# A hybrid encoder step: input in two pieces with weights between, the pool mixer's products one group later, parameters turned inside a chunk

## The chip, the cores and the metric

The kernel runs on one core of one Trainium2 chip, as one launch. The metric is the device time of an execution in microseconds (us), the median of several runs. Beside it stands one profiled execution, whose trace is read here: its span runs from the first to the last instruction.

## The reference

One layer of a streaming encoder trunk, for 256 prompt frames of a new stream and 32 frames of a running one (288 positions in all), model width 2048, in float32:

```python
def run_layer(x, pos, hist_pool, hist_sconv, h0, hist_fconv, p):
    xn = rmsnorm(x, p['norm_mix_pre'])
    proj = xn @ p['w_in']
    u, z, xbc, dt_raw = proj[..., :o1], proj[..., o1:o2], proj[..., o2:o3], proj[..., o3:]
    y_pool, new_pool = pool_mixer(u, ...)    # 4 groups of 256 channels, trailing means over 2/4/8/16
    y_ssd, new_sconv, new_h = ssd_mixer(z, xbc, dt_raw, ...)   # conv, chunked scan, gate, grouped norm
    mix = jnp.concatenate([y_pool, y_ssd], axis=-1) @ p['w_out']
    x = x + rmsnorm(mix, p['norm_mix_post'])
    up, new_fconv = causal_dwconv(rmsnorm(x, p['norm_ffn_pre']) @ p['w_up'], ...)
    gate, val = up[..., :D_FF], up[..., D_FF:]
    f = (jax.nn.silu(gate) * val) @ p['w_down']
    return x + rmsnorm(f, p['norm_ffn_post']), new_pool, new_sconv, new_h, new_fconv
```

In the pool mixer each group takes its trailing mean less `u` and multiplies it by a 256 x 256 matrix, `y = einsum('bsgc,gcd->bsgd', d, w_pool)`. The outputs are the new frames and the states.

## The kernel before

Activations lie transposed, channels on the 128 partitions and the 288 positions along the row. A K tile is 128 input channels; there are 16 of them at the input. Each weight and each activation is split into a high and a low part, and one product of the mathematics is three on TensorE (PE): high x high, high x low, low x high (`mm3`, L162 to L164). ScalarE (ACT) makes the high part of a weight (`whi`, L156), VectorE (DVE) the low part (`wlo`, L157), four buffers each.

The instructions of each engine run in order. A planner that models the engines sets that order, except for the instructions marked `pin` or `keep_in_program_order`, which hold the order of the program; `high_priority` moves an instruction ahead in the plan.

**The head.** The 800 columns of `w_in` that are needed first (some `u`, B, C and dt) are computed chunk by chunk over K: `CHUNKS` has ten chunks, c0 to c3 of one K tile each and c4 to c9 of two. The first four K tiles come in by rows and are turned on PE (`turn_first`). The other twelve come in three pieces of four K tiles (`input_load(1)` to `(3)`, L238, four loads each, one for each 32 partitions), with rows of 128 words, and the sample rows in four loads (L262). Channels are dealt to K tiles with a step of four (`j=4`), so that DVE can turn a tile from these pieces (L386). All these loads and the weights of a chunk (`first_load`, two loads, L244 and L245) are issued by one engine, SP, in the order of the program: c0, c1, c2, c3, input piece 1, sample rows, c4, c5, input pieces 2 and 3, c6 to c9.

`prepare(i)` makes chunk i ready: on ACT the high part of the weights (L382, L383), the high part of `xn` (L391), and for some chunks squares of the input (L417); on DVE the turned input (L386), the low part of the weights (L396) and of `xn` (L398). It is called one chunk ahead. Then come the chunk's products (L483): 20 for a chunk of one tile, 40 for one of two.

In front of the products of c5, c6 and c7 a block of parameters is turned on PE (`columns`, L328) and copied by ACT (L434, L437, L440); the FFN's parameters are turned before products 0 and 24 of c8 (L475). All these use one buffer in turn, since the other two of its pool hold sums: a turn waits for the copy of the one before.

**The pool mixer.** Projections of 256 columns follow one another (`project`, 96 products). At the end of the mixer stage:

```python
for n, i in enumerate((2, 1, 0)):
    ps = ups.pop() if n == 0 else project(win, [(256 * i, 256)], xn, K16)
    for j in range(2):
        pool_in(2 * i + j, ps[j])
    pool_tile(2 * i + 2)
    pool_tile(2 * i + 3)
    pool_group(i + 1)
    for t in range(8 + 3 * n, min(11 + 3 * n, NX)):
        tc.keep_in_program_order(dve.tensor_tensor(xs[t], xs[t], rg[1], op=ALU.mult))
```

`pool_in` takes a projection's result out of PE's memory, `pool_tile` makes the window sums and the split `du` on DVE and ACT (L884 to L891, L120, L121), and `pool_group` multiplies two `du` tiles by the group's matrix (12 products) and splits the result for the output projection (L124, L125). Beside this runs the norm factor `rg[1]` of the second SSD group (a square root, L768, and a reciprocal, L769). The output projection starts with the SSD's tiles (`mixs`) and ends with the pool's (`mixp`).

Of the kernel before, what the change touches and what calls it, by code (L numbers as in the profile page):

```python
# [8 lines left out]
F32 = mybir.dt.float32  # L9
# [7 lines left out]
P = 128  # L17
# [3 lines left out]
NS = 32  # L21
# [28 lines left out]
def body(  # L50
# [57 lines left out]
    def aux(shape, name):  # L108
        return aux_ps.tile(shape, F32, tag="aux", name=name)
# [115 lines left out]
    xsv = x_sample.rearrange("o t (c i w) -> i (o t) c w", i=4, w=P)  # L225
# [9 lines left out]

    def input_load(c):
        for i in range(4):
            pin(sp.dma_start(out=xt[NS * i : NS * (i + 1), 0:8, c - 1, :], in_=xpv[i][:, :, c, :]))  # L238

    def first_load(kb, n):  # L240

        raw = wpool.tile([P, n, NW], F32, tag="raw", name="raw")
        src = win0[:, kb : kb + n] if kb < 4 else win[:, kb // 4, kb % 4 : kb % 4 + n]
        pin(sp.dma_start(out=raw[:, :, 2 * P :], in_=src[:, :, O_B : O_B + NW - 2 * P]))  # L244
        pin(sp.dma_start(out=raw[:, :, : 2 * P], in_=src[:, :, D_POOL - 2 * P : D_POOL]))  # L245
        raws.append(raw)
# [41 lines left out]
    for i in range(NE):  # L288
# [2 lines left out]
        ebuf.append(e)  # L291

    pool.dma_start(
        out=g_mix_pre[:, 4:].rearrange("p (c j) -> p c j", j=4),
        in_=norm_mix_pre[0, 4 * P :].rearrange("(c p j) -> p c j", p=P, j=4),
    )
    ubuf = []
    for i in range(4):
# [36 lines left out]

    xn = []
    xT = []
    xT_d = dram.tile([4, P, 4, NT], F32, name="xT_d")
# [15 lines left out]
    spots = xin.tile([P, 9, NS], F32, name="spots")  # L354
    pf = const.tile([P, 6, NF * 2], F32, name="pf")
    copies = []
    last_split = []

    def turn_first(t):
# [7 lines left out]
    def prepare(i, p_=None):  # L367

        kb, n = CHUNKS[i]
        raw = raws.pop(0)  # L370

        w = xin.tile([P, n, 2 * NW + HEADS], F32R, tag="w", bufs=3, name="w")
        hi, lo = w[:, :, :NW], w[:, :, NW : 2 * NW]
        tiles = range(kb, kb + n)
        pieces = (slice(2 * P, 4 * P), slice(4 * P, NW), slice(0, 2 * P)) if i == 0 else (slice(0, NW),)
        for t in tiles:
            xT.append(btile("xT"))
            xn.append(atile("xn"))
        if i == 0:
            pin(act.activation(xn[0][:, 0, :], p_, AF.Copy, scale=g_mix_pre[:, 0:1]))  # L380
        for c in pieces:
            pin(act.activation(hi[:, :, c], raw[:, :, c], AF.Copy))  # L382
        pin(act.activation(w[:, :, 2 * NW :], raw[:, :, NB:], AF.Copy))  # L383
        for t in tiles:
            if p_ is None:
                pin(dve.transpose(  # L386
                    xT[t].rearrange("p (b t) -> p b t", t=NS),
                    xt[:, :, t // 4 - 1, :].rearrange("p b (f j) -> p b f j", j=4)[:, :, :, t % 4],
                ))
            if i:  # L390
                pin(act.activation(  # L391
                    xn[t][:, 0, :], xT[t] if p_ is None else p_, AF.Copy, scale=g_mix_pre[:, t : t + 1]
                ))
        if i:
            for c in pieces:
                pin(dve.tensor_tensor(lo[:, :, c], raw[:, :, c], hi[:, :, c].bitcast(F32), op=ALU.subtract))  # L396
        for t in tiles:
            pin(dve.scalar_tensor_tensor(  # L398
                xn[t][:, 1, :], xT[t] if p_ is None else p_, g_mix_pre[:, t : t + 1], xn[t][:, 0, :].bitcast(F32),
                op0=ALU.mult, op1=ALU.subtract,  # L400
            ))
        if p_ is not None:
            for c in pieces if i == 0 else ():
                pin(dve.tensor_tensor(lo[:, :, c], raw[:, :, c], hi[:, :, c].bitcast(F32), op=ALU.subtract))
            pin(dve.tensor_copy(xT[kb], p_))
        if i + 4 < len(CHUNKS):
            first_load(*CHUNKS[i + 4])
        if i == 1:
            input_load(2)
            input_load(3)  # L410
        if 1 <= i <= 3:
            b = i - 1
            src = x0[:, b] if b < 2 else x0s
            n_ = src.shape[0]
            pin(act.activation(junk[:n_], src, AF.Square, accum_out=ssum[:n_, 9 + b : 10 + b]))
        for b in SQUARES.get(i, ()):
            pin(act.activation(  # L417
                junk[:, : 3 * P].rearrange("p (c w) -> p c w", w=P), xt[:, b], AF.Square, accum_out=ssum[:, b : b + 1]
            ))
        return w  # L420

# [6 lines left out]
    for i, (kb, n) in enumerate(CHUNKS):  # L428
        if 4 <= i + 1 < len(CHUNKS):
            ahead_w.append(prepare(i + 1))  # L430

        if i == 5:
            pb = columns(pb_in, 108, "pb", copies)
            pin(act.activation(*copies.pop(), AF.Copy))  # L434
        if i == 6:
            pa = columns(pa_in, 124, "pa", copies)
            pin(act.activation(*copies.pop(), AF.Copy))  # L437
        if i == 7:
            pc = columns(pc_in, 120, "pc", copies)
            pin(act.activation(*copies.pop(), AF.Copy))  # L440
        if i == len(CHUNKS) - 1:

            pool.tensor_tensor(
# [25 lines left out]
        for q, (r, m, k, x) in enumerate(products):  # L469
            if i < 3 and q == (6 if i else 12):  # L470
                ahead_w.append(prepare(i + 1, turn_first(i + 1)))
            if i == 8 and q in (0, 24):
                p_ = aux([P, 3, NF * 2], "ptf")
                for j in range(3):
                    pin(pe.transpose(p_[:, j, :], pf_in[:, q // 8 + j, :], ident[: NF * 2, : NF * 2]))  # L475
                pin(act.activation(pf[:, q // 8 : q // 8 + 3, :], p_, AF.Copy))
# [6 lines left out]
            pin(pe.matmul(out, c, xn[kb + k][:, x, :], start=kb + k + r + x == 0, stop=kb + k == KD - 1 and stop))  # L483
    early.close()
    ahead[0] = 200
    g_mix_post = pb[:, 60:76]
    g_ffn_pre = pb[:, 76:92]
    g_ffn_post = pb[:, 92:108]
# [66 lines left out]
        pool_in(NU - 2 + i, first[i])  # L555

    xs_ps = [project(win, [(O_X, 256)], xn, K16, wait=last_split)]
    xT_f = xT_d.rearrange("c p j n -> (c p j) n")
    for t in range(KD):
        pin(sp.dma_start(out=xT_d[t // 4, :, t % 4, :] if t > 3 else xT_f[t * P : (t + 1) * P, :], in_=xT[t]))  # L560
    xs_in = {}


# [446 lines left out]
    for grp in ((0, 1), (2,), (3,), (4,), (5,), (6,), (7,)):  # L1010
# [7 lines left out]
        elif grp[0] == 6:  # L1018
            late_in[:] = [state_in(t, t >= LATE + 4) for t in range(LATE, NX - 2)]
        if grp[0] == 0:  # L1020
            sp.dma_start(out=xT, in_=xT_d.rearrange("c p j n -> (c p j) n").rearrange("(k q) n -> q k n", q=P))
# [334 lines left out]
```

## Time and profile before

| what | value |
|---|---|
| median of 3 runs | 1366.51 us (1365.96 to 1369.6) |
| profiled execution, its own time | 1366.29 us |
| its span | 1364.6 us |
| mean granted TensorE clock | 0.994 |
| PE / DVE / ACT / POOL busy | 98% / 65% / 49% / 17% |
| bytes moved by DMA, mean rate | 252.15 MB, 185 GB/s |

A row of the timeline is: start and length in us, engine, line, operation, output and inputs, count, and in brackets the idle time before it and what ended it. The granted clock is the share of full speed at which TensorE ran. A line number is that of the kernel before; a helper's line stands for all its callers, so the names of tiles tell them apart.

### The profile page before, as it was taken

What the parts mean: (1) busy time and instruction counts of PE and PEld (TensorE: products, weight loads), DVE (VectorE), ACT (ScalarE), POOL (GpSimd) and SP (SyncE); (2) the same over time, 40 slices, a digit from 0 to 9 for tenths busy, and PEclk for the clock granted to TensorE, in tenths of its full rate; (3) what the DMA queues carried; (4) which work ended last, traced back from release to release, by engine and by line L of the source; (5) the groups of instructions that cost most, each with busy time, mean ns of one, the idle gap of its engine ahead of it and who ended that gap; (6) DMA issues with size and microseconds to landing.
All of it is one profiled execution on the core that took longest, in us unless ns stands there. A gap on an engine that the chain in (4) does not pass through costs nothing.

```text
span 1364.6 us, 25783 instructions
## 1 busy us (share of the span) xinstructions
PE 1340.9 (98%) x10183; PEld 1329.1 (97%) x10183; DVE 892.5 (65%) x1510; ACT 671.7 (49%) x1029; POOL 231.9 (17%) x395
## 2 busy tenths in 40 slices
PE   8999999989999999999999999999999999999997
PEld 7999999979999999999999999999999999999996
DVE  6799979768634469977766643335666666664444
ACT  5656957535444356644444443334444444454442
POOL 4121112211232330211211100000211111101110
PEclk9999999999999999999999999999999999999999
DMA  9879887555755654877555455555455554576763
GB/s 260 253 199 256 242 247 205 149 163 180 228 174 183 184 153 139 251 198 198 168 160 181 147 170 170 160 168 175 156 173 167 161 176 158 166 233 179 199 172 91
DMA packets 302945, 252.15 MB, mean 185 GB/s; under 512 B 74708, under 2 KB 295410, under 8 KB 302822
## 3 DMA queue, kind: packets, MB, share of 16 engines
q1 hardware_dynamic: 300414, 245.76, 59.8%
q0 software_dynamic: 2352, 4.66, 1.2%
q8 instruction: 80, 1.31, 0.4%
q14 instruction: 43, 0.35, 0.1%
q10 hardware_dynamic: 56, 0.07, 0.0%
HBM read 236.13 MB, written 14.31 MB: 184 GB/s over the span
## 4 chain that ended last, share of the span: by engine, by line
PE 90%; DMA 5%; DVE 2%; SPq 1%; issue 1%; ACT 1%; DVEq 0%; ACTq 0%
PE acc L162 28%; PE acc L164 28%; PE acc L163 28%; DMA xs_d<-blocks 2%; PE acc L483 1%; DMA xk<-xs_d 1%; PE pst L986 1%; DMA raw<-in_w_in 1%; DMA xt<-in_x_prompt 1%; DVE wlo L157 1%; PE acc L1262 1%; SPq L202 0%; PE acc_x L483 0%; DMA xt<-in_x_sample 0%; PE py L713 0%
## 5 line engine op out<-in xcount | busy, mean ns | idle before, releaser
L157 DVE TENSOR_TENSOR wlo<-raw,whi 128x1024 fp32r<-128x1024 f32 (+1 forms) x402 | 479.1, 1194 | 349.3 <-ACT whi L156 348.4
L156 ACT ACTIVATE whi<-raw 128x1024 fp32r<-128x1024 f32 (+1 forms) x402 | 413.4, 1031 | 485.0 <-PE acc L163 414.4
L162 PE MATMUL acc<-hn,whi 128*128 128x288 f32 x1376 | 404.1, 295 | 0.0
L163 PE MATMUL acc<-hn,whi 128*128 128x288 f32 x1376 | 403.6, 294 | 0.2 <-DVE hn L1045 0.2
L164 PE MATMUL acc<-hn,wlo 128*128 128x288 f32 x1376 | 403.1, 294 | 0.0
L163 PEld LDWEIGHTS acc<-hn,whi 128*128 128x128 f32 x1376 | 259.7, 189 | 0.7 <-DVE hn L1045 0.7
L164 PEld LDWEIGHTS acc<-hn,wlo 128*128 128x128 f32 x1376 | 259.6, 189 | 0.0
L162 PEld LDWEIGHTS acc<-hn,whi 128*128 128x128 f32 x1376 | 257.2, 187 | 0.1
L162 PE MATMUL acc<-fa,whi 128*128 128x288 f32 x682 | 201.9, 296 | 0.0
L163 PE MATMUL acc<-fa,whi 128*128 128x288 f32 x682 | 201.9, 296 | 0.0
L164 PE MATMUL acc<-fa,wlo 128*128 128x288 f32 x682 | 201.5, 295 | 0.0
L162 PE MATMUL acc<-xn,whi 128*128 128x288 f32 x608 | 181.8, 299 | 0.2 <-DVE ebuf L514 0.2
L164 PE MATMUL acc<-xn,wlo 128*128 128x288 f32 x608 | 179.8, 296 | 1.9 <-DVE wlo L157 1.9
L163 PE MATMUL acc<-xn,whi 128*128 128x288 f32 x608 | 180.0, 296 | 0.0
L163 PEld LDWEIGHTS acc<-fa,whi 128*128 128x128 f32 x682 | 128.6, 188 | 0.0
L162 PEld LDWEIGHTS acc<-fa,whi 128*128 128x128 f32 x682 | 128.1, 188 | 0.0
L164 PEld LDWEIGHTS acc<-fa,wlo 128*128 128x128 f32 x682 | 127.9, 188 | 0.0
L164 PEld LDWEIGHTS acc<-xn,wlo 128*128 128x128 f32 x608 | 115.7, 190 | 2.2 <-DVE wlo L157 2.2
L163 PEld LDWEIGHTS acc<-xn,whi 128*128 128x128 f32 x608 | 115.9, 191 | 0.1
L162 PEld LDWEIGHTS acc<-xn,whi 128*128 128x128 f32 x608 | 114.9, 189 | 0.9 <-issue 0.4
L1080 POOL COPY fc_stage<-ebuf 128x4 f32<-128x4 f32 x88 | 26.7, 303 | 498.0 <-DVE ebuf L1079 498.0
L1086 DVE SCALAR_TENSOR_TENSOR fc<-ebuf,pf,fc 128x290 f32<-128x290 f32 x176 | 90.4, 517 | 3.6 <-ACT fc L1084 1.0
(355 smaller groups left out, 1774.1 us busy)
## 6 DMA issues: line engine op xcount, KB each, us to landing
raw<-in_w_up SPq DMA_DIRECT2D x80, 1024.0 KB, 5.2
raw<-in_w_in SPq DMA_DIRECT2D x76, 512.0 KB, 5.0
raw<-in_w_down SPq DMA_DIRECT2D x32, 1024.0 KB, 5.3
raw<-in_w_out SPq DMA_DIRECT2D x24, 1024.0 KB, 5.5
raw<-in_w_down SPq DMA_DIRECT2D x16, 768.0 KB, 4.8
raw<-in_w_up SPq DMA_DIRECT2D x14, 512.0 KB, 4.2
gb<-g_d SPq DMA_DIRECT2D x8, 832.0 KB, 6.8
raw<-in_w_in SPq DMA_DIRECT2D x6, 544.0 KB, 6.8
```

The lines of the kernel that those rows point to most:

```text
L156: act.activation(hi, raw[:, k : k + n, :], AF.Copy)
L157: dve.tensor_tensor(lo, raw[:, k : k + n, :], hi.bitcast(F32), op=ALU.subtract)
L162: then(pe.matmul(out, wh, a[:, 0, :], start=start, stop=False))
L163: then(pe.matmul(out, wh, a[:, 1, :], start=False, stop=False))
L164: then(pe.matmul(out, wl, a[:, 0, :], start=False, stop=stop))
L483: pin(pe.matmul(out, c, xn[kb + k][:, x, :], start=kb + k + r + x == 0, stop=kb + k == KD - 1 and stop))
L986: ins = pe.matmul(st[:, o, :], x_, btok[:, gi, b, :], start=b != 1, stop=b != 0)
L1080: pool.tensor_copy(fc_stage[:, :, :, i], e[:, 256:324].rearrange("p (s c) -> p s c", c=34)[:, :, 0:2])
L1086: dve.scalar_tensor_tensor(c, e[:, r_ : r_ + 290], pf[:, r_, i : i + 1], c, op0=ALU.mult, op1=ALU.add)
L1262: pin(pe.matmul(o, hi, f2[k][:, :, c], start=k == 0, stop=end, skip_group_check=True))
```

## The change

The twelve K tiles come in two pieces of six. Rows of a piece have 192 words, channels are dealt with a step of six, and the loads, the gains, the scratch copy `xT_d` and `fetch_w` (which reads 2 and 6 K tiles instead of 4 and 4 in its second half) follow that. The first piece and the sample rows are issued ahead of the weights of c3; the second piece stands where pieces 2 and 3 stood. The parameter blocks are turned at product 12 of c5, c6 and c7, and at products 12 and 30 of c8. The products of pool group 3 move behind the next projection.

```diff
-                for k in range(kb, kb + nk, 4):
-                    src = view[:, k // 4] if k else win0
-                    sp.dma_start(out=raw[:, k - kb : k - kb + 4, :], in_=src[:, :, c0 : c0 + nc_])
+                for k0, k1, src in ((0, 4, win0), (4, 10, view[:, 0]), (10, KD, view[:, 1])):
+                    a, b = max(k0, kb), min(k1, kb + nk)
+                    if a < b:
+                        sp.dma_start(out=raw[:, a - kb : b - kb, :], in_=src[:, a - k0 : b - k0, c0 : c0 + nc_])
...
-    xt = xin.tile([P, 9, 3, P], F32, name="xt")
-    xpv = x_prompt.rearrange("o (b t) (c i w) -> i t (o b) c w", t=NS, i=4, w=P)
-    win = w_in.rearrange("o (c p j) w -> p (o c) j w", p=P, j=4)
+    xt = xin.tile([P, 9, 2, 192], F32, name="xt")
+    xpv = x_prompt[0, :, 4 * P :].rearrange("(b t) (c i w) -> i t b c w", t=NS, i=4, w=192)
+    win = w_in[0, 4 * P :, :].rearrange("(c p j) w -> p c j w", p=P, j=6)
...
     first_load(*CHUNKS[2])
+    input_load(0)
+    for i in range(4):
+        pin(sp.dma_start(out=xt[NS * i : NS * (i + 1), 8, :, :], in_=xsv[i]))
     first_load(*CHUNKS[3])
-    input_load(1)
-    for i in range(4):
-        pin(sp.dma_start(out=xt[NS * i : NS * (i + 1), 8, :, :], in_=xsv[i, :, 1:4, :]))
...
         if i == 1:
-            input_load(2)
-            input_load(3)
+            input_load(1)
...
-        if i == 5:
-            pb = columns(pb_in, 108, "pb", copies)
-            pin(act.activation(*copies.pop(), AF.Copy))
...
+            if i in (5, 6, 7) and q == 12:
+                src, m_, name = ((pb_in, 108, "pb"), (pa_in, 124, "pa"), (pc_in, 120, "pc"))[i - 5]
+                params[name] = columns(src, m_, name, copies)
+                pin(act.activation(*copies.pop(), AF.Copy))
-            if i == 8 and q in (0, 24):
+            if i == 8 and q in (12, 30):
...
+        if n == 1:
+            pool_group(3)
         pool_tile(2 * i + 2)
         pool_tile(2 * i + 3)
-        pool_group(i + 1)
+        if n:
+            pool_group(i + 1)
```

More of the change, by code (lines that the diff above doesn't have):

```diff
@@ L222, in body @@
     x0s = wpool.tile([NS, 4 * P], F32, tag="lo", name="x0s")
[L223 to L226 removed]
+    xt = xin.tile([P, 9, 2, 192], F32, name="xt")
+    xpv = x_prompt[0, :, 4 * P :].rearrange("(b t) (c i w) -> i t b c w", t=NS, i=4, w=192)
+    xsv = x_sample[0, :, 4 * P :].rearrange("t (c i w) -> i t c w", i=4, w=192)
+    win = w_in[0, 4 * P :, :].rearrange("(c p j) w -> p c j w", p=P, j=6)
     win0 = w_in[0, 0 : 4 * P, :].rearrange("(k p) w -> p k w", p=P)
@@ L237, in input_load @@
         for i in range(4):
-            pin(sp.dma_start(out=xt[NS * i : NS * (i + 1), 0:8, c - 1, :], in_=xpv[i][:, :, c, :]))
+            pin(sp.dma_start(out=xt[NS * i : NS * (i + 1), 0:8, c, :], in_=xpv[i][:, :, c, :]))
     def first_load(kb, n):
         raw = wpool.tile([P, n, NW], F32, tag="raw", name="raw")
-        src = win0[:, kb : kb + n] if kb < 4 else win[:, kb // 4, kb % 4 : kb % 4 + n]
+        src = win0[:, kb : kb + n] if kb < 4 else win[:, (kb - 4) // 6, (kb - 4) % 6 : (kb - 4) % 6 + n]
         pin(sp.dma_start(out=raw[:, :, 2 * P :], in_=src[:, :, O_B : O_B + NW - 2 * P]))
@@ L293, in body @@
     pool.dma_start(
-        out=g_mix_pre[:, 4:].rearrange("p (c j) -> p c j", j=4),
-        in_=norm_mix_pre[0, 4 * P :].rearrange("(c p j) -> p c j", p=P, j=4),
+        out=g_mix_pre[:, 4:].rearrange("p (c j) -> p c j", j=6),
+        in_=norm_mix_pre[0, 4 * P :].rearrange("(c p j) -> p c j", p=P, j=6),
     )
@@ L337, in body @@
     xT = []
-    xT_d = dram.tile([4, P, 4, NT], F32, name="xT_d")
+    xT_d = dram.tile([D_MODEL, NT], F32, name="xT_d")
     first = [aux([P, NT], "acc_x") for _ in range(2)]
@@ L356, in body @@
     copies = []
+    params = {}
     last_split = []
@@ L387, in prepare @@
                     xT[t].rearrange("p (b t) -> p b t", t=NS),
-                    xt[:, :, t // 4 - 1, :].rearrange("p b (f j) -> p b f j", j=4)[:, :, :, t % 4],
+                    xt[:, :, (t - 4) // 6, :].rearrange("p b (f j) -> p b f j", j=6)[:, :, :, (t - 4) % 6],
                 ))
@@ L417, in prepare @@
             pin(act.activation(
-                junk[:, : 3 * P].rearrange("p (c w) -> p c w", w=P), xt[:, b], AF.Square, accum_out=ssum[:, b : b + 1]
+                junk[:, : 3 * P].rearrange("p (c w) -> p c w", c=2), xt[:, b], AF.Square, accum_out=ssum[:, b : b + 1]
             ))
@@ L430, in body @@
             ahead_w.append(prepare(i + 1))
-        if i == 5:
-            pb = columns(pb_in, 108, "pb", copies)
[L434 to L440, printed above, removed]
         if i == len(CHUNKS) - 1:
@@ L471, in body @@
                 ahead_w.append(prepare(i + 1, turn_first(i + 1)))
-            if i == 8 and q in (0, 24):
+            if i in (5, 6, 7) and q == 12:
[3 more added lines that the diff above has]
+            if i == 8 and q in (12, 30):
                 p_ = aux([P, 3, NF * 2], "ptf")
+                o = 0 if q == 12 else 3
                 for j in range(3):
-                    pin(pe.transpose(p_[:, j, :], pf_in[:, q // 8 + j, :], ident[: NF * 2, : NF * 2]))
-                pin(act.activation(pf[:, q // 8 : q // 8 + 3, :], p_, AF.Copy))
+                    pin(pe.transpose(p_[:, j, :], pf_in[:, o + j, :], ident[: NF * 2, : NF * 2]))
+                pin(act.activation(pf[:, o : o + 3, :], p_, AF.Copy))
             if r is None:
@@ L485, in body @@
     ahead[0] = 200
+    pb, pa, pc = params["pb"], params["pa"], params["pc"]
     g_mix_post = pb[:, 60:76]
@@ L557, in body @@
     xs_ps = [project(win, [(O_X, 256)], xn, K16, wait=last_split)]
-    xT_f = xT_d.rearrange("c p j n -> (c p j) n")
+    xT_v = xT_d[4 * P :, :].rearrange("(c p j) n -> p c j n", p=P, j=6)
     for t in range(KD):
-        pin(sp.dma_start(out=xT_d[t // 4, :, t % 4, :] if t > 3 else xT_f[t * P : (t + 1) * P, :], in_=xT[t]))
+        to = xT_v[:, (t - 4) // 6, (t - 4) % 6, :] if t > 3 else xT_d[t * P : (t + 1) * P, :]
+        pin(sp.dma_start(out=to, in_=xT[t]))
     xs_in = {}
@@ L1020, in body @@
         if grp[0] == 0:
-            sp.dma_start(out=xT, in_=xT_d.rearrange("c p j n -> (c p j) n").rearrange("(k q) n -> q k n", q=P))
+            sp.dma_start(out=xT, in_=xT_d.rearrange("(k q) n -> q k n", q=P))
             state_out(sc_stage.rearrange("p s r t -> p s (r t)"), 60, (rows4(new_sconv_p), rows4(new_sconv_s)), op_)
```

## The prediction

> **What bounds the kernel now.** I read the page first: busy time of the engines and the shares of the chain that ended last.
>
> ```profile
> span 1364.6 us, 25783 instructions
> ...
> PE 1340.9 (98%) x10183; PEld 1329.1 (97%) x10183; DVE 892.5 (65%) x1510; ACT 671.7 (49%) x1029; POOL 231.9 (17%) x395
> ...
> PE 90%; DMA 5%; DVE 2%; SPq 1%; issue 1%; ACT 1%; DVEq 0%; ACTq 0%
> ```
>
> TensorE (PE) is the bound: it is busy for 1340.9 of 1364.6 us. Only its 23.7 us without work, and time at a lower clock, can be won by moving things, and that is all that this change does. The view of waits, kept to PE, says where that idle time lies; columns are total, times, longest.
>
> ```profile
> PE acc L162 <- ACT du L120: 6.8, 1, 6.8
> PE pt L328 <- ACT pb L434: 3.4, 1, 3.4
> PE acc L164 <- DVE wlo L157: 1.9, 1, 1.9
> PE acc L483 <- DVE xn L398: 1.0, 1, 1.0
> ```
>
> The two longest are single events, and the change touches both: the pool mixer's first products (L162 on `du`, 6.8 us) and the turning of a parameter block (L328 on the copy of `pb`, 3.4 us). I then read the timeline around each.
>
> **The head: input, weights, parameters.** Chunk c6 is K tiles 8 and 9. These are its rows, from several engines (start, length):
>
> ```profile
> 30.90 1.54 ACT L382 ACTIVATE w<-raw 128x1600 fp32r<-128x1600 f32 x1 [6.05 <-DMA raw<-in_w_in]
> 31.33 0.69 PE L483 MATMUL acc<-xn,w 128*64 128x288 f32 x4
> 32.48 1.83 DVE L396 TENSOR_TENSOR w<-raw,w 128x1600 fp32r<-128x1600 f32 x1 [4.72 <-ACT w L382]
> 34.22 0.94 DVE L398 SCALAR_TENSOR_TENSOR xn<-xT,g,xn 128x288 fp32r<-128x288 f32 x2
> 35.14 0.24 ACT L434 ACTIVATE pb<-pt 128x108 f32<-128x108 f32 x1
> 35.44 0.33 PE L328 MATMUL pt<-ident,pa_in 124*128 124x124 f32 x1 [3.42 <-ACT pb L434]
> 35.52 4.97 PE L483 MATMUL acc<-xn,w 128*128 128x288 f32 x24
> ...
> 42.45 0.27 PE L328 MATMUL pt<-ident,pc_in 120*128 120x120 f32 x1
> 42.48 3.41 PE L483 MATMUL acc<-xn,w 128*128 128x288 f32 x24
> ```
>
> PE ends chunk c5 at 32.0 and stands until 35.4. The named releaser is the copy of `pb`, but that copy is queued on ACT behind c6's own preparation, which waited 6.05 us for c6's weights to land at 30.9. So two things must be undone. Without the parameter turn in front, c6's second product needs the low half of `xn`, which DVE has for the first tile at 34.22 + 0.94/2 = 34.7: landing plus 3.8 us. Its first steady product now comes at about 35.7 (the `pa` turn, then the products). The mid-chunk turn alone wins 35.7 - 34.7 = 1.0 us; the rest needs earlier weights. In the changed order the copy of `pb` still follows c6's preparation on ACT, but its reader, the `pa` turn, comes 12 products into c6, landing + 3.8 + 12 x 0.14 = landing + 5.5, and the copy ends at 35.38 = landing + 4.5: hidden by 1.0 us, and if that cover goes the wait returns with at most the old 0.3 to 1 us. The later turns (`pc`, and `pf` at products 12 and 30) have a whole chunk, or 18 x 0.14 = 2.5 us, between copy and reader: nothing.
>
> The stall costs more than itself. The windows view has the granted clock in the third column from the end:
>
> ```profile
> 20.00:21.00 1.00, 0.20 (x2) 0.00 (x0) 1.00 (x2) 0.00 (x0) 0.00 (x0) 1.00 1.21 172
> 37.00:38.00 1.00, 1.00 (x6) 1.00 (x6) 1.00 (x1) 1.00 (x3) 0.00 (x0) 0.50 1.10 377
> ```
>
> After the 3.4 us stall the clock is 0.50; in the 1.0 us stall at 20 to 21 it stays 1.00. c6's first 24 products took 4.97 us, c7's 3.41: 1.5 us lost at half clock. A gap well under 3.4 us should save that too.
>
> When do c6's weights land in the new order? The DMA view of three stretches (22:25, 29:35, 303.7:304.7) gives packets, bytes and rate, and the page's issue list gives the input loads:
>
> ```profile
> DMA packets 1214, 0.60 MB, mean 202 GB/s; under 512 B 88, under 2 KB 1203, under 8 KB 1214
> ...
> DMA packets 1488, 2.26 MB, mean 377 GB/s; under 512 B 83, under 2 KB 773, under 8 KB 1488
> ...
> DMA packets 621, 0.32 MB, mean 320 GB/s; under 512 B 54, under 2 KB 621, under 8 KB 621
> ```
>
> ```profile
> xt<-in_x_prompt SPq DMA_DIRECT2D x12, 128.0 KB, 9.4
> ...
> xt<-in_x_sample SPq DMA_DIRECT2D x4, 48.0 KB, 5.3
> ```
>
> The input runs at 202 GB/s (22:25), weights at 377 (29:35). The bytes ahead of c6 stay the same: 12 x 128 + 4 x 48 = 1728 KB, 1.77 MB, become 8 x 192 + 4 x 48. At 202 GB/s they take 8.8 us. Only the rows get longer, 512 to 768 bytes. Two rows bound that: no gain (202), or the 320 GB/s which 515-byte packets reach at 303.7, 5.5 us, 3.2 us earlier. Below nothing: longer rows give no reason, and 16 loads become 12. But the stretch at 303.7 moves the blocks of `btok`, which span 128 partitions, while each input load lands in 32 partitions, before and after. So short rows alone are not the limit, and I stay near the no-gain end: 0.6 us, c6 lands at 30.3 (27.7 to 30.9). [...]
>
> What pays for this is c3, K tile 3. Its weights are now issued behind the first input piece and the sample rows:
>
> ```profile
> 6.29 0.43 SPq L245 DMA_DIRECT2D raw<-in_w_in  x1
> ...
> raw<-in_w_in SPq DMA_DIRECT2D x1, 128.0 KB, 4.8
> ...
> 16.99 2.02 PE L483 MATMUL acc<-xn,w 128*64 128x288 f32 x14
> ```
>
> They landed at 6.29 + 4.8 = 11.1. With 4 x 192 + 4 x 48 = 960 KB (0.98 MB) ahead at 202 GB/s, 4.9 us, they land at about 16.0; weight split, `lo` and the low half of `xn` put the second product of c3 at about 18.3. In before c3 starts some two products into the row at 16.99, at 17.25: PE waits about 1 us (0 to 2), clock unharmed. 256 KB more input also stands ahead of c4 and c5 (1.3 us at 202), so c4's wait of 1.0 grows by about as much or is merged with it, and c5 ends at about 33 instead of 32. This is covered: c6 is ready at 30.3 + 3.8 = 34.1. Without the cover it would cost that 1.0.
>
> Head: start of c6 35.7 to 34.1, 1.6 us; clock, 1.4 us (the idle gap is 33 to 34, about 1 us): **3.0 us**, from 1.0 (no rate gain, clock falls all the same) to 4.9 (landing at 27.7, then c5's end at 32 to 33 sets it). c7 to c9 keep their pace: c7 starts 6.8 us after c6 now, 5.4 then, against ACT and DVE steps of 4.4 us per chunk. The transposes with a step of six words, the gain load in 24-byte runs and the `xT_d` stores keep their counts and end before c6's weights; the 2+6 split of a weight load is four issues as before. All nothing.
>
> **The pool mixer.** The second place, in the timeline:
>
> ```profile
> 299.93 1.06 ACT L156 ACTIVATE whi<-raw 128x1024 fp32r<-128x1024 f32 x1 [2.11 <-PE acc L163]
> 300.30 0.38 PE L863 MATMUL pso<-ident,sc_stage 128*60 128x128 f32 x2
> 302.83 1.95 DVE L769 RECIPROCAL rg<-rg 128x288 f32<-128x288 f32 x1 [0.18 <-ACT rg L768]
> 307.01 0.44 ACT L120 ACTIVATE du<-dpool 128x288 fp32r<-128x288 f32 x1 [3.89 <-DVE dpool L890]
> 307.51 0.85 PE L162 MATMUL acc<-du,whi 128*128 128x288 f32 x2 [6.83 <-ACT du L120]
> 308.16 0.44 PE L162 MATMUL acc<-xn,whi 128*128 128x288 f32 x1
> ...
> 313.11 0.29 PE L163 MATMUL acc<-du,whi 128*128 128x288 f32 x1
> ...
> 316.40 0.45 DVE L121 TENSOR_TENSOR du<-dpool,du 128x288 fp32r<-128x288 f32 x1
> ```
>
> PE is in order. The products of group 3 head its queue and need `du`, which DVE makes only after the window sums and a 1.95 us reciprocal; the next projection's products (`xn`) sit behind them, ready. The idle is 6.83 us, and from 307.51 to 313.11 PE ran 23 matmuls in 5.60 us at half clock, for which, at the (3.41 - 0.3)/23 = 0.136 us a product of the row at 42.48, 3.1 us would do: 2.5 lost. In the new order the projection's 96 products (96 x 0.136 = 13.0 us) come first. Their weights are there: the split at 299.93 is its third of four, and the fourth takes over the buffer of the first products that end. Removed: 6.8 + 2.5 = **9.3 us**.
>
> What is late next: groups 3 and 2 now stand together at 300.5 + 13.0 = 313.5, and group 2 at 315.1. Its last `du` came at 316.40 + 0.45, with the extra weight splits ahead of it (1.2 + 0.7 + 0.7 us of DVE) at up to 318: a wait of 0 to 3 us, and behind it in PE's queue stands the last projection. The windows of 300 to 350 give the other limit, DVE's sum:
>
> ```profile
> sum 50.00, PE 43.17 PEld 42.72 DVE 45.23 ACT 27.42 POOL 11.07; mean PE 4.32 PEld 4.27 DVE 4.52 ACT 2.74 POOL 1.11
> ```
>
> PE without the loss crosses this stretch in 50 - 9.3 = 40.7 us, and DVE has 45.2 us of work in it. 4.5 us must slide past it, which it can as far as it is not wanted at once (splits of `xs` and of the pool's results for the output projection). I give 2.0 us back (0 to 5, the 4.5 and a little). Net **7.3 us**.
>
> **Sum.** 3.0 + 7.3 = 10.3 us. The profiled execution took 1366.29 us (span 1364.6 and 1.7 around it), 0.2 under the median of 1366.51, so 1366.3 - 10.3 = 1356.0.
>
> **The rivals.** *Row length was the limit* (0.15): the input goes at 300 GB/s or more, c6 lands at 28, PE has no gap there: 1366.3 - 4.9 - 8 = 1353.4. For it: 320 GB/s elsewhere; against: 32 partitions per load. *DVE's backlog comes back as one stall* (0.14): 4.5 us in one piece before group 2, long enough for 2.5 us of half clock behind it: 1366.3 - 3.0 - 9.3 + 7.0 = 1361.0, and 1363 if the head also gives less. For it: DVE is full from 325 to 340; against: the order has ready products to put between. *The change does not do what it says* (0.08): the order of the queues is planned by a model of the engines, and it had `du` ready 6.8 us before the chip did; it can place group 2, or another product, as wrongly, with the same price. Head only: 1363.3. *Slower* (0.08): the same backlog paid at half clock in three places, at group 2, at group 1 and at the first output products, each a stall of 4 us with 2.5 us of slow clock: 19.5 - 9.3 - 3.0 = 7.2 us, 1373.5. It decides once each of the three exceeds the stall after which the clock falls (somewhere between 1.0 and 3.4 us); against it stands that only 4.5 us of DVE work is over.
>
> **How the numbers follow.** My forecast has 0.55, its own range 1353 to 1359. A measurement of this kernel can tell about 0.3%, 4.1 us. Faster by more: the forecast, the first rival and 0.10 of the backlog case, 0.80. Within: 0.04 of the backlog case and the 0.08 of a new misplaced product, 0.12. Slower: 0.08. The range runs from 1351.0, the first rival with both upper bounds (4.9 + 9.3 = 14.2 would be 1352.1) and a little of the 1.9 us wait on `wlo`, to 1363.5, which takes in the one-stall and head-only cases.
>
> **What would show it.** Right: no PE wait on `du` above 3 us; clock 1.00 from 300 to 315; no wait of the turns (L328's line) on `pb`; c6's weights split at about 30.3 and its products 1.6 us earlier, 24 of them in 3.4 us; a new wait of about 1 us before c3 or c4. Wrong: the input rate at 300 GB/s or the split of c6 before 29; a stall over 3 us between 313 and 345 with a clock of 0.50 after it; PE waits on the early weights that add up to more than 3 us.

## The result, and the profile after

| | us |
|---|---|
| before, median of 20 runs | 1365.93 (1359.08 to 1370.01) |
| after, median of 20 runs | 1362.01 (1358.32 to 1366.71) |
| ratio | 0.9971, 95% interval 0.9957 to 0.9984 |
| profiled execution of after | 1359.29, span 1357.6, clock 0.997 |

The change wins 3.9 us; 10.3 were forecast. 1362.0 lies in the range (1351.0 to 1363.5), at its slow end. The profiled execution of after is one of the fast ones of its kernel: 7.0 us less than that of before, where the medians differ by 3.9. Lines of after are numbered one to three off from before (`wlo` L158, `mm3` L163 to L165, the head's products L480).

From the page of after, PE's busy time and the chain by engine:

```profile
PE 1340.9 (99%) x10183; PEld 1328.9 (98%) x10183; DVE 891.2 (66%) x1510; ACT 671.5 (49%) x1029; POOL 235.5 (17%) x395
...
PE 91%; DMA 4%; DVE 2%; ACT 1%; SPq 1%; issue 1%; DVEq 0%; ACTq 0%
```

The bound is the same; what moved are the waits. PE's waits of after (total, times, longest):

```profile
PE acc L165 <- DVE wlo L158: 3.1, 1, 3.1
PE acc L480 <- DVE xn L400: 2.4, 3, 1.0
PE acc L163 <- ACT du L120: 2.0, 1, 2.0
```

The 6.8 us on `du` and the 3.4 us on `pb` are gone. Back came 2.0 us on another `du`, 1.4 us more in front of early chunks, and the wait on `wlo` grew from 1.9 to 3.1 us. Rows of the timeline of after, head first:

```profile
30.64 1.54 ACT L384 ACTIVATE w<-raw 128x1600 fp32r<-128x1600 f32 x1 [4.04 <-DMA raw<-in_w_in]
34.53 1.75 PE L480 MATMUL acc<-xn,w 128*128 128x288 f32 x11 [0.85 <-DVE xn L400]
58.16 0.37 PE L163 MATMUL acc<-xn,whi 128*128 128x288 f32 x1 [0.17 <-DVE ebuf L512]
...
199.17 0.96 DVE L689 TENSOR_TENSOR xw<-xk,tok 128x768 f32<-128x768 f32 x1 [2.36 <-DMA xk<-xs_d]
203.98 0.40 PE L165 MATMUL acc<-xn,wlo 128*128 128x288 f32 x1 [3.06 <-DVE wlo L158]
```

In this one trace the head looks nearly as forecast (c6 split at 30.6 for 30.3, steady products at 34.5 for 34.1, clock 1.00 from 0 to 40) and the first projection product comes 2.5 us earlier than before's 60.69. But the sums over the first SSD group (`psum_t`) start at 244.5, before at 244.4. The 2.5 us were lost between 201 and 208: VectorE waits for the reload of `xk` from DRAM, `wlo` is queued behind, PE stands 3.06 us, and the clock falls (third column from the end of the windows view, here of after):

```profile
203.00:208.00 5.00, 4.02 (x19) 4.02 (x20) 5.00 (x9) 2.44 (x3) 0.00 (x0) 0.67 0.59 188
300.00:314.00 14.00, 14.00 (x106) 13.88 (x105) 13.65 (x33) 6.69 (x9) 3.94 (x7) 1.00 0.88 282
315.00:321.00 6.00, 4.01 (x19) 3.90 (x19) 6.00 (x16) 2.05 (x4) 1.70 (x2) 0.72 0.93 277
```

The second and third rows are the pool mixer: no wait up to 314, then 1.99 us of wait and about 1.7 us lost at half clock behind it (0.72 over 6 us). The first `mixs` product moved from 339.8 to 334.2.

### The profile page after: what moved, and what is told of

It reads as the page before. It is cut to its first block, busy times and chain, and to the rows that moved or that the text cites. A ratio compares the mean times of both kernels' runs of the same rounds, so it can differ in the third digit from the quotient of the medians.

```text
span 1357.6 us, 25774 instructions
## 1 busy us (share of the span) xinstructions
PE 1340.9 (99%) x10183; PEld 1328.9 (98%) x10183; DVE 891.2 (66%) x1510; ACT 671.5 (49%) x1029; POOL 235.5 (17%) x395
## 3 DMA queue, kind: packets, MB, share of 16 engines
q8 instruction: 80, 1.31, 0.4%
## 4 chain that ended last, share of the span: by engine, by line
PE 91%; DMA 4%; DVE 2%; ACT 1%; SPq 1%; issue 1%; DVEq 0%; ACTq 0%
PE acc L163 28%; PE acc L165 28%; PE acc L164 28%; PE acc L480 2%; DMA xs_d<-blocks 1%; DMA xk<-xs_d 1%; PE pst L988 1%; PE acc_x L480 1%; DMA raw<-in_w_in 1%; PE acc L1264 1%; ACT m L696 1%; DMA xt<-in_x_prompt 0%; SPq L203 0%; DVE wlo L158 0%; DMA h<-in_state_ssd 0%
## 5 line engine op out<-in xcount | busy, mean ns | idle before, releaser
L158 DVE TENSOR_TENSOR wlo<-raw,whi 128x1024 fp32r<-128x1024 f32 (+1 forms) x402 | 479.1, 1194 | 344.7 <-ACT whi L157 343.7
L163 PE MATMUL acc<-hn,whi 128*128 128x288 f32 x1376 | 404.1, 295 | 0.0
L165 PE MATMUL acc<-hn,wlo 128*128 128x288 f32 x1376 | 403.2, 294 | 0.0
L165 PEld LDWEIGHTS acc<-hn,wlo 128*128 128x128 f32 x1376 | 259.6, 189 | 0.0
L163 PEld LDWEIGHTS acc<-hn,whi 128*128 128x128 f32 x1376 | 257.2, 187 | 0.1
L163 PE MATMUL acc<-fa,whi 128*128 128x288 f32 x682 | 202.0, 296 | 0.0
L165 PE MATMUL acc<-fa,wlo 128*128 128x288 f32 x682 | 201.5, 295 | 0.0
L165 PE MATMUL acc<-xn,wlo 128*128 128x288 f32 x608 | 180.0, 296 | 3.1 <-DVE wlo L158 3.1
L163 PE MATMUL acc<-xn,whi 128*128 128x288 f32 x608 | 182.3, 300 | 0.2 <-DVE ebuf L512 0.2
L163 PEld LDWEIGHTS acc<-fa,whi 128*128 128x128 f32 x682 | 128.1, 188 | 0.0
L165 PEld LDWEIGHTS acc<-fa,wlo 128*128 128x128 f32 x682 | 127.9, 187 | 0.0
L165 PEld LDWEIGHTS acc<-xn,wlo 128*128 128x128 f32 x608 | 115.9, 191 | 3.3 <-DVE wlo L158 3.3
L163 PEld LDWEIGHTS acc<-xn,whi 128*128 128x128 f32 x608 | 115.3, 190 | 0.9 <-issue 0.4
```

What stands on the lines that cost most here:

```text
L158: dve.tensor_tensor(lo, raw[:, k : k + n, :], hi.bitcast(F32), op=ALU.subtract)
L163: then(pe.matmul(out, wh, a[:, 0, :], start=start, stop=False))
L165: then(pe.matmul(out, wl, a[:, 0, :], start=False, stop=stop))
```

## Experiments

Times are ratios to the kernel before, run beside each, with the 95% interval in brackets.

**The two halves alone.** The pool mixer's lines only; then all but them.

```diff
+        if n == 1:
+            pool_group(3)
         pool_tile(2 * i + 2)
         pool_tile(2 * i + 3)
-        pool_group(i + 1)
+        if n:
+            pool_group(i + 1)
```

> The kernel before with the pool mixer's group move alone. Theory A (the mixer's gain comes through whole, less a 2.0 us wait on du and 1.7 us of half clock behind it; the head's gain is the part that is lost): head and psum_t at about 244.4 as before, first mixs product 5 to 6 us earlier (339.8 to about 334.2), end 5 to 6 us earlier, 1360.3. Rival B (the mixer's gain needs the earlier head, or is given back at the output projection): mixs 5 us earlier, but end less than 3 us earlier, 1363 or more.

> The kernel before with all the head's edits (two input pieces, weights between them, parameters turned mid-chunk), pool mixer's groups as before. Theory A (the head's gain is real and is swallowed at about 200 us by VectorE's wait for the reload of xk, the PE wait on wlo growing from 1.9 to 3.1 us with 1.5 us of half clock behind it): first projection product 2.5 us earlier (60.7 to 58.2), first psum_t within 0.5 us of 244.4, end within 1 us of the kernel before, 1365.9. Rival C (the head's gain reaches the end and only scatter of the runs hid it): psum_t at about 242 and end 2.5 us earlier, 1363.4.

The mixer alone: 0.9955 (0.9938 to 0.9972), 6.2 us. The head alone: 0.9993 (0.9979 to 1.0007), 1.0 us (-1.0 to 2.9), which cannot be told from zero. Theory A's ends held, but not its reason for the head: in the head's run the first projection product came 1.6 us earlier, not 2.5, and `psum_t` at 245.6 (245.8 in the mixer's run), not at 244.4. In the mixer's run, with the head of before, the first projection product came at 58.09, as early as in after. That did not help, since PE then waited 4.39 us where before waits 1.92, and about 1.7 us more were lost at half clock behind it (0.83 from 200 to 210):

```profile
205.45 0.61 PE L164 MATMUL acc<-xn,wlo 128*128 128x288 f32 x1 [4.39 <-DVE wlo L157]
```

So one and the same head ends 2.6 us apart in two executions, and the head's 2.5 us in the pair of traces above may be scatter alone.

**The head in parts.** Turns mid-chunk with the loads of before, and the reverse.

> The kernel before with the parameters turned mid-chunk alone (input loads and pool mixer as before). So far the weights of c6 were split at 30.9 and 29.9 us with the input order of before, and at 30.6, 31.5, 32.0 and 32.9 with the changed order, so Theory H: the two input pieces land c6 about 1.4 us later, which eats what the turns win. It expects here: split of c6 at 29.8 to 31.0, no PE wait on pb, c6's first steady product 3.8 us behind its split, no half clock, first projection product at 57.3 to 58.5 (60.7 and 58.1 seen with the turns as before). Rival S (the order of the input costs nothing, and the later c6 was scatter): the same here, so this run tells only the size of the turns; the end 0 to 2 us earlier than the kernel before, since most of it is lost again at the wait on wlo at about 203.

> The kernel before with the input in two pieces and the weights between them, the parameters turned at the chunks' fronts as before. Theory H (768-byte rows move no faster, and c6 lands later): input rate 150 to 215 GB/s from 22 to 26 us, split of c6 at 31 to 33 us, PE waits for pb again (1 to 2.5 us), first projection product at 59.5 to 62, end the same as before or 1 to 2 us later. Rival S (the order of the input lands c6 at 30.3 or earlier, the rest was scatter): split of c6 at or before 30.3, first projection product before 59, end not later than before.

0.9988 (0.9976 to 1.0001) and 0.9999 (0.9987 to 1.0011). With the profiles of the other runs that share a head (the split of c6 is the start of ScalarE's copy of its weights, for whose landing it waits):

| input order | turns | split of c6 | first projection product |
|---|---|---|---|
| before | before | 30.90, 29.87 | 60.69, 58.09 |
| before | mid-chunk | 30.76, 30.70, 31.19, 30.89, 30.98 | 58.30, 58.24, 58.75, 58.44, 60.05 |
| changed | before | 31.90 | 60.13 |
| changed | mid-chunk | 30.64, 31.54, 31.98, 32.91, 31.51 | 58.16, 59.07, 59.52, 60.99, 59.05 |

On the mean the changed order splits c6 at 31.7, the old one at 30.8: 1.0 us later, not 0.6 earlier. The turns win 0.6 (59.4 to 58.8), the order gives it back (59.4). That is theory H. The later split stands on seven profiles against six; the 0.6 us of the turns rests on two profiles with the old turns that lie 2.6 us apart, and is not shown.

The input's own rate is best read from 10 to 12 us, where nearly all packets are input: first before, with rows of 512 bytes, then after, with 768.

```profile
DMA packets 838, 0.40 MB, mean 201 GB/s; under 512 B 86, under 2 KB 830, under 8 KB 838
DMA packets 621, 0.42 MB, mean 208 GB/s; under 512 B 73, under 2 KB 618, under 8 KB 621
```

Over the profiles of the table the means are 194 and 202 GB/s, a difference no larger than the spread within each order (184 to 205, 192 to 215). So the longer rows moved at most a little faster, and c6 is late for another reason. Up to 28 us both orders had moved about as much (6.5 to 7.0 MB with the old order, 6.4 to 6.7 with the changed one). But before the split of c6 four of the six profiles with the changed order had moved 7.9 to 8.1 MB, the other two and all seven with the old one 7.5 to 7.7: bytes that c6 does not need went ahead of its last ones. Which these are, and why, is open.

**The reload of `xk`.** Two buffers and a higher priority; then, with two buffers again, the load moved to where the quad before ends (the edit shown).

```diff
 def ssd_first(q):
+        xk = mp.tile([P, 3, 2 * P], F32, tag="xk", bufs=2, name="xk")
+        ... (its two loads, taken out of ssd_quad)
         gb = mp.tile([P, 4, MW], F32, tag="gb", bufs=2, name="gb")
```

> The changed kernel with two buffers for xk and its reload issued ahead of the weight loads. Theory A (the reload is what swallows the head's gain): VectorE's wait of 2.4 us for xk before 199.2 gone or under 0.5, PE's wait on wlo at 200 to 204 under 1.0 us, clock 1.00 behind it, psum_t 3 to 4 us earlier (244.5 to about 241), end about 3.5 us earlier than the changed kernel, 1358.5. Rival D (VectorE's own work is the bound between 100 and 245 us, where it is about 88% busy): the wait on wlo comes back elsewhere before 245, psum_t within 0.7 us of 244.5, time as the changed kernel, 1362.0.

> The changed kernel with xk in two buffers and its reload issued a whole quad ahead, beside gb and the state. Theory A (the reload holds VectorE, and wlo behind it, at about 183 and 199 us; that wait and the half clock behind it swallow what the head wins): VectorE's waits for xk (11.4 us in 4) under 2 us in all, no PE wait on wlo over 1 us between 60 and 250, clock 1.00 from 200 to 250, psum_t at 241 to 242, end 3 to 5 us earlier than the changed kernel, 1357 to 1359, and a smaller scatter. Rival D (VectorE's work and the DMA queues are full there, and another wait takes its place): psum_t within 1 us of 244.5, the wait on wlo 2 us or more, end 1361 to 1363.

Priority gave 0.9930 (0.9907 to 0.9953), though its profiled execution took 1365.0 us, with a wait on `wlo` of 4.54 us: that trace bears out nothing of theory A. The earlier load gave 0.9919 (0.9902 to 0.9936), 11 us under before, and its clock from 200 to 250 stayed whole (its wait on `wlo`, then the windows view):

```profile
PE acc L165 <- DVE wlo L158: 1.3, 1, 1.3
```

```profile
200.00:250.00 50.00, 48.69 (x399) 47.37 (x398) 45.65 (x70) 34.42 (x66) 10.63 (x9) 1.00 0.65 186
```

`psum_t` came at 242.1, near theory A's 241 to 242, and rival D's figures missed. But so did A's: the wait on `wlo` was over 1 us, and VectorE's waits for `xk` fell only from 11.4 to 8.3 us. At the place that A names nothing moved: the load was issued at 192.40 (192.42 in after), and VectorE waited 2.56 us for it (2.36). Gone are earlier waits, 1.56 us at 135 and 1.6 of the 2.34 at 164, and `wlo` came free 0.8 us earlier, at 203.17; the rest of the shorter wait is PE's later arrival. So the runs show that the edit wins time, but this trace does not show that it does so by theory A; nor do the two runs tell the second buffer from the earlier issue. With the old input order and the mid-chunk turns in the same kernel:

> The reload of xk a quad ahead, the pool mixer's move and the mid-chunk turns, but the input in three pieces and in the order of the kernel before: beside the run with the reload ahead it differs in the input alone. Theory H (the two pieces land c6 later and win nothing): split of c6 at 29.8 to 31.0 as in the three profiles with this order (30.9, 29.9, 30.8; five with the changed order gave 30.6 to 32.9), first projection product 57.5 to 58.5 against 59.4 on the mean of the changed order, end 0 to 2 us earlier than the run with the reload ahead (0.9919 of before), 1354 to 1355.5. Rival S (the new order wins): end 1 us or more later than it, above 1356.5.

0.9918 (0.9902 to 0.9933). `psum_t` at 239.7, no wait on `wlo` left, and VectorE's waits for `xk` down to 3.6 us; its end is the same within the interval, so H's 0 to 2 us are not shown at the end.

All profiles together say more than the single ones. Where the reload was as before, PE waited 1.65 to 4.39 us on `wlo` at this place (eight profiles, the run with the higher priority left aside); with it a quad ahead 1.31 to 2.21 us with the changed input order (four), and 0.3 us or less with the old one (four). From the first projection product to `psum_t` these groups took 183.4 to 187.7, 183.1 to 185.5 and 181.5 to 182.2 us. So the reload ahead does shorten the wait. The changed input order seems to cost 1 us or more here, behind the head; that is not shown, since three of its four profiles belong to kernels that also load the input by two queues (described next), and the ends do not tell the orders apart. One edit that the prediction put at nothing lies in this stretch, the split of `fetch_w`'s loads into 2 and 6 K tiles; no run has it alone.

**What holds the input's rate.** Loads over all partitions; two queues; two queues later; two queues on the two halves.

```diff
-        for i in range(4):
-            pin(sp.dma_start(out=xt[NS * i : NS * (i + 1), 0:8, c, :], in_=xpv[i][:, :, c, :]))
+        for b in range(8):                                      # first run
+            pin(sp.dma_start(out=xt[:, b, c, :], in_=xpv[:, :, b, c, :]))
+        # last run: SP loads i = 0, 1 of piece 2; in prepare(3), behind c3's work:
+        #   act.dma_start(...) for i = 2, 3
```

> The changed kernel with each input piece loaded in eight loads of 128 partitions (96 KB) in place of four loads of 32 partitions (192 KB); rows of 768 bytes in both, the same bytes. Theory P (the 32 partitions of a load hold the rate at about 200 GB/s): the stretch from 20 to 27 us moves 300 GB/s or more, split of c6 at 28 to 29 us, c3's wait shorter too, first projection product at about 56 to 57. Rival R (row length or the strided source holds the rate): 150 to 220 GB/s as before, split of c6 at 30.6 to 33, first projection product 58 to 61. The end is about the changed kernel's in both, since the wait on wlo at about 203 stands after it; 0 to 3 us less by P.

> The run with the reload ahead, the second input piece's four loads on two queues in turn (SP's and ACT's), so that two groups of 32 partitions fill at once; the same bytes, rows and loads. Theory P (a group of 32 partitions holds a load at about 200 GB/s while all 16 engines are busy; 128-partition loads that had four engines in use moved 91 GB/s, 22.7 an engine with the same 768-byte rows, as much as the weights' 23.4): the stretch from 20 to 26 us moves 300 GB/s or more, split of c6 1.5 to 3 us earlier than 31.8, at 29 to 30.3, first projection product at 56 to 57.5. Rival R (the source's strided rows hold the rate): 150 to 220 GB/s, split of c6 at 30.6 to 33. End 0 to 2 us earlier than the run with the reload ahead by P, the same by R.

> The run with the reload ahead (changed input order), the second input piece split between two queues as before, but ScalarE's two loads issued behind its work on c3, at about 18 us, so that they stand beside SP's two and not ahead of the early weights. Theory P (32 partitions hold a load at about 200 GB/s, two groups at once pass twice that): where input alone moves (20 to 24 us, 150 to 200 GB/s in the profiles so far) 280 GB/s or more, split of c6 at 29 to 30.5, first projection product at 56.5 to 58. Rival R (something else holds the input's rate, such as its strided rows): 200 GB/s or less there, split of c6 at 30.6 or later. End 1354 to 1356 in both.

> As the run before, but SP loads the second piece's partitions 0 to 63 and ScalarE's queue 64 to 127 (before: 0 to 31 and 64 to 95 on SP, the two others on ScalarE, so that the pairs in flight together were neighbours). The run before moved 191 GB/s from 21 to 25 us with both queues at work. Theory P2 (neighbouring groups share one limit, the two halves of the partitions have one each): 21 to 25 us at 280 GB/s or more, split of c6 at 29 to 30.5 us. Rival R (the source's rows hold the rate): 160 to 220 GB/s, split of c6 at 31 to 33. [...] End 1356 to 1360 in both.

The wide loads gave 1.0006 (0.9995 to 1.0017). Their input moved at 91 GB/s and took 27.7% of the time of 16 DMA engines, as much as between four and five engines can give (27.7% of 16 is 4.4; first row, the mean of 26 to 30 us; second row, the share). Four is also the size of the outermost dimension of their source; that this is the reason was not tested, and so the run says nothing for or against theory P. The first try with two queues, 0.9959 (0.9940 to 0.9979), issued ScalarE's half at 10.3 us, ahead of c3's weights, and does not bear on the question. The other two differ in the program only in which groups fly together: neighbours (third row) or one from each half of the partitions (fourth), both from 21 to 25 us.

```profile
DMA packets 484, 0.36 MB, mean 91 GB/s; under 512 B 16, under 2 KB 484, under 8 KB 484
q1 hardware_dynamic: 484, 0.36, 27.7%
```

```profile
DMA packets 858, 0.76 MB, mean 191 GB/s; under 512 B 83, under 2 KB 803, under 8 KB 858
```

```profile
DMA packets 968, 0.96 MB, mean 241 GB/s; under 512 B 82, under 2 KB 811, under 8 KB 968
```

c6 was split at 31.84 and 29.68, the latter the earliest of all profiles with the changed order; ends 0.9935 (0.9918 to 0.9952) and 0.9927 (0.9904 to 0.9950). This speaks for a limit that neighbouring groups share, but 241 is under the 280 expected, weights moved in both stretches and more of them in the second (157 packets over 2 KB against 55), and it is one profile each: not shown.

**The 2.0 us in front of group 2.** Multiplications of `xs` moved away; the right ones; then `du` ahead of group 3's evacuations.

```diff
-        for t in range(8 + 3 * n, min(11 + 3 * n, NX)):
+        for t in ((8, 9, 10), (), (11, 12, 13, 14, 15))[n]:     # first and second run
+        for t in ((), (8, 9, 10, 11, 12), (13, 14, 15))[n]:     # third and fourth
...                                                              # fourth alone: pool_tile ahead of pool_group(3), and in pool_group:
+                if i == 3:
+                    order.enter_context(tc.issue_after(du_at[-1].ins))
```

> The changed kernel with the three multiplications of xs by rg that stand on VectorE at 313.4 to 314.6, ahead of group 2's last du, moved behind the next projection. Theory A (those 1.25 us and the queue behind them set the 2.0 us wait on du, and the 1.7 us of half clock is its price): wait on du below 1.0 us, clock 1.00 from 315 to 322, first mixs product 2 to 3 us earlier than the changed kernel, end 2 to 3 us earlier, 1359.5. Rival D (VectorE's total backlog counts there, not its order): the wait goes to wlo or mixs a little later, first mixs product within 0.7 us, 1362.0.

> The same with the three multiplications of xs by rg behind the next projection as well. If the 2.0 us wait before group 2's last products was theirs, it goes and the first mixs product comes 2 us earlier than in the run before it, 1352 to 1353. If it is the queue of weight splits (the wait stayed at 2.0 us, on wlo in place of du, when these three were moved alone), nothing: the same time within 1 us, the wait at 2.0 us.

> The run with the old input order, the mid-chunk turns, the reload of xk ahead and the pool mixer's move, now with the multiplications of xs tiles 8 to 10 by rg (three on VectorE, 1.25 us, right ahead of the last window sums of group 2; the earlier attempt moved tiles 11 to 13, which stand elsewhere) issued after group 2. Theory A (VectorE's queue sets the 2.0 us wait before group 2's last products): the wait falls to about 0.7 us, the clock stays 1.00 behind it in every profile, first mixs product 1.2 to 3 us earlier than 329.4, end 1352.5 to 1354.5 (0.990 to 0.991 of before). Rival E (ScalarE's queue sets it: two weight copies and a mixp copy stand ahead of du): wait 1.9 us or more, end 1355 to 1356.

> The run before this, with group 2's window sums issued ahead of group 3's evacuations, and these (two mixp copies on ScalarE) held until the last du of group 2 is copied. In eight profiles PE's wait before group 2's last products was 1.99 us, whatever VectorE did, also where dpool was ready 1.2 us earlier; the row on ScalarE behind PE's last product of group 3 was the same each time: mixp 0.50, weight copy 1.05, mixp 0.49, du 0.44, which with a 0.21 us wait and the overlap of neighbours is 2.2 us to PE's next product. Theory E (that row on ScalarE sets it): the wait falls under 1.0 us, no half clock behind it, first mixs product 1 to 3 us earlier than 330.1, end 1352 to 1353.7. Rival F (the low half of the next weights on VectorE ends at the same moment and sets it as well): the wait stays at 1.5 us or more, with wlo as its releaser, end 1354 to 1355.

0.9950 (0.9930 to 0.9969), 0.9913 (0.9897 to 0.9929), 0.9906 (0.9888 to 0.9925), 0.9905 (0.9890 to 0.9921). The first two moved tiles 11 to 13, which do not stand at that place: they test nothing of it, and the wait was 1.99 us. The third had VectorE's last window sum ready 1.1 us earlier, counted from PE's last product, and the wait was 1.99 us again. It also decides between `du` and `wlo`. In seven of the twelve profiles with this wait the view names `wlo` as the releaser, in five `du`; in after and in the mixer's run the two end within 0.1 us of each other. In the third run they are apart:

```profile
310.16 1.21 DVE L157 TENSOR_TENSOR wlo<-raw,whi 128x1024 fp32r<-128x1024 f32 x1
312.04 0.44 ACT L120 ACTIVATE du<-dpool 128x288 fp32r<-128x288 f32 x1
312.54 0.54 PE L162 MATMUL acc<-du,whi 128*128 128x288 f32 x2 [1.99 <-ACT du L120]
```

`wlo` ended there at 311.37, and PE waited for `du` to its end at 312.48. ScalarE's timeline in after and in the fourth run, and that run's wait:

```profile
314.88 0.50 ACT L124 ACTIVATE mixp<-acc,pa 128x288 fp32r<-128x288 f32 x1 [0.21 <-PE acc L165]
315.28 1.05 ACT L157 ACTIVATE whi<-raw 128x1024 fp32r<-128x1024 f32 x1
316.23 0.49 ACT L124 ACTIVATE mixp<-acc,pa 128x288 fp32r<-128x288 f32 x1
316.61 0.44 ACT L120 ACTIVATE du<-dpool 128x288 fp32r<-128x288 f32 x1
```

```profile
312.78 1.06 ACT L156 ACTIVATE whi<-raw 128x1024 fp32r<-128x1024 f32 x1 [0.39 <-ACT so L863]
313.74 0.43 ACT L893 ACTIVATE du<-dpool 128x288 fp32r<-128x288 f32 x1
```

```profile
PE acc L162 <- ACT du L893: 1.4, 1, 1.4
```

`du` is the last of a row on ScalarE that starts with PE's own last product of group 3; hence the constant 1.99. With the two `mixp` copies taken out of that row the wait is 1.40: theory E, though not under 1.0, since the weight copy still stood ahead. The end did not move further. 0.9905 of before is where these edits end, against 0.9971 for after: some 9 us less.

## Why the prediction was right and wrong, by its steps

What failed is the head: 3.0 us were forecast, and alone it won 1.0 (-1.0 to 2.9). Of its three terms the earlier landing of c6 did not come, and the half clock was there to be saved in only one of three profiles with the old turns. The mixer, forecast at 7.3, won 6.2 alone (3.8 to 8.5).

- **The rate of the input (0.6 us of the head's 3.0)** failed, and with it the statement that a loss is excluded. The 0.6 us was the author's choice between no gain and 3.2 us, and no run shows it: rows of 768 bytes moved hardly faster (202 GB/s against 194 on the mean of 10 to 12 us), and c6 came 1.0 us later on the mean. The forecast took the landing from the rate and the bytes ahead of c6; in four of six profiles other bytes went ahead too. Why is open.
- **The mid-chunk turns (1.0 us)** were right in mechanism: no wait on `pb`, the later turns cost nothing. c6's steady products came 3.9 us behind its split in the three runs read for this (after, the head's, the turns'), where 3.8 were forecast. The gain measured 0.6 us on the mean of few profiles, which is not shown.
- **The price at c3 (about 1 us, 0 to 2)** was 0.75 us in after and 2.3 us in the head's own run.
- **The clock (1.4 us)** hangs on the execution: in a second profile with before's head the wait on `pb` was 1.75 us and the clock 1.00 from 28 to 40, in the profile with the changed loads and the old turns the wait was 1.72 us and the 24 products behind it took 3.42 us (c7's in before, at full clock, 3.41), so that there was nothing to save in either. The forecast read one trace's 3.4 us stall as the kernel's.
- **That a gain in the head reaches the end** was never argued, and in the mixer's run an early head was lost at the wait on `wlo`. That wait stood in the forecast's first table as a remainder of 1.9 us; with the reload as before it is 1.65 to 4.39 us from profile to profile. The kernel with the reload a quad ahead is some 7 us faster than after by the ratios (0.9919 and 0.9971), more than the head was to win.
- **The removed part of the mixer (9.3 us)** was right: from 300 to 314 PE ran without a wait at a clock of 1.00 in after; in the mixer's run the clock was 1.00 from 300 to 340.
- **The give-back (2.0 us)** was right in size, 1.99 us of wait, and wrong in cause: not VectorE's 4.5 us of backlog but ScalarE's row. The half clock behind it, left at nothing, costs 1.7 us where it falls. From `psum_t` to the first `mixs` product before took 95.4 us; 88.1 in the mixer's own run, where the clock held (7.3 won, the forecast net), 89.7 in after, where it fell (5.7). The other profiles agree: 94.4 to 95.4 us in the four without the move, 88.1 to 88.7 in the seven with it whose clock held, 89.7 to 90.2 in the five where it fell.

Sum: mixer 6.2 and head 1.0, each alone, against 7.3 and 3.0. Measured with both 3.9 (2.2 to 5.9). The two halves' intervals allow it; what became of the other 3 us is not shown. That 1362.0 lies in the range is no credit to the sum: the range reached that far for the one-stall and the head-only case, and neither came.

The forecast took one profile of before as its typical course, and put the stall behind which the clock falls between 1.0 and 3.4 us. The length of a stall alone does not decide it: behind the same wait of 1.99 us the clock fell in 5 of 12 profiles.

## What to carry to other kernels

Before pricing a gain early in the kernel, follow it to the next place where PE waits for something that does not move with it, and price that wait with the gain taken off: a small wait behind a reload from DRAM can swallow it (1.92 us on `wlo` in before, 4.39 in the mixer's run, where the head ended 2.6 us earlier). A wait in one trace is one draw (1.65 to 4.39 us here with the same reload); for terms of 1 to 3 us take several profiles. When a wait keeps its length while other things move (1.99 us here in 12 profiles), look on another engine for a chain that starts at the waiting engine's own last result.

## What was not expected of the hardware

The clock fell after the stall of 1.99 us in 5 of 12 profiles. At the wait on `wlo` it fell after 1.83, 2.21, 2.44, 3.06, 3.2, 3.25, 4.39 and 4.54 us, and held after 1.92, 1.70, 1.65 and 1.31 us. So from 1.8 to 2.0 us the length did not decide. The loss was 1.5 to 1.7 us each time, except behind the 4.54 us: there 1.6 us were lost up to 210 (0.84 from 200), and products still came 0.24 us apart. The mean clocks of 20 executions of after lie between 0.994 and 0.998; over 1360 us that is, as an estimate, some 5 of the 8 us by which these executions differ. Loads into 128 partitions, from a source whose outermost dimension is 4, moved 91 GB/s on 27.7% of the DMA engines' time (26 to 30 us), while loads into 32 partitions at a time moved 194 and 202 GB/s (means of 10 to 12 us, by the two orders); the reason is not shown.
